# Quartered products: seven products of sums of quarters for eight, weight sums by adding DMAs, and a token-major residual, in a two-layer decoder trunk in float32

## The chip, the cores and the metric

The kernel runs on one core of a Trainium2 chip. TensorE (PE in the rows; its weight loads are PEld) multiplies, VectorE (DVE), ScalarE (ACT) and GpSimd (POOL) work element by element, and SyncE (SP) issues most transfers, which 16 DMA engines carry. The metric is the device time of one execution in microseconds (us), the median of several runs.

## The reference, cut to what matters

There are 512 tokens of width 1024 and two layers. One layer is:

```python
h = rms_norm(x, norm_mix_g[l])
proj = h @ w_in[l]                      # 1024 x 7168: pool 512, q 512, k 512, v 1024, gate 1024, xq 512, 3 branch gates of 1024
y_ret = retention(rq, rk, rv, rg, positions, ret_norm_g[l])       # 4 heads, decaying causal scores, rotary q and k
y_mem = memory_attention(xq, rms_norm(mem, mem_norm_g[l]), w_mem_kv[l])   # 4 heads over 256 memory tokens
y_pool = pool_mixer(pool_u, pool_w[l], pool_scale[l])             # trailing means over 2, 4, 8, 16 tokens
merged = sum over b of sigmoid(gate_b) * (y_b @ w_up_b[l])        # w_up_ret 1024 x 1024, the other two 512 x 1024
x = x + merged @ w_out[l]                                         # 1024 x 1024
h2 = rms_norm(x, norm_mlp_g[l])
x = x + square(relu(h2 @ w_mlp1[l])) @ w_mlp2[l]                  # 1024 x 4096 and 4096 x 1024
```

After the second layer comes a last RMS norm. All data are float32.

## The kernel before

**Exact products in three passes.** Each float32 operand is split into a high part, rounded to the type fp32r that TensorE takes in one pass, and the rest. `split_w` does it for weights: ACT writes `wh` (L120) and DVE `wl = raw - wh` (L121), for 1024 columns at a time. `split` (L99, L100; with a scale L102, L103) does it for activations. `mm` then issues three matmuls for each pair of tiles:

```python
(sh, sl), (mh, ml) = stat, mov
nc.tensor.matmul(ps, sh, mh, start=start, stop=False)     # L127
nc.tensor.matmul(ps, sh, ml, start=False, stop=False)     # L128
nc.tensor.matmul(ps, sl, mh, start=False, stop=stop)      # L129
```

The stationary tile is 128x128; the moving tile has up to 512 columns, and the result goes to one of 8 PSUM banks of 128x512.

**Feature-major products.** The activations lie as 8 tiles `hh`, `hl` of 128 features by 512 tokens. `proj_fm` takes the columns of a weight in groups of 128: per group one bank and, for a depth of 1024, 8 x 3 matmuls with the weights stationary and 512 tokens moving. A product of the whole 1024 x 1024 takes 8 x 8 x 3 = 192 of them:

```python
for j in range(step // P):
    ps = bank()
    for r, raw in enumerate(raws):
        wp = split_w(raw[:, :, j * P:(j + 1) * P])
        for k in range(raw.shape[1]):
            kk = r * 8 + k
            mm(ps[:, :n], tuple(p[:, k, :] for p in wp), xs[kk], kk == 0, kk == kt - 1)
    late.append((c // P + j, ps))
    yield
    if len(late) > lag:
        done(*late.pop(0))
```

`proj_tm` gives token-major results (values, memory values, and the last product), with 128 tokens stationary and 512 weight columns moving. `done` is what follows a bank: the row factor of the norm, the gate, the relu and square (L716, L717, and the split with POOL at L100), or the addition to the residual `xT` (L703), which stays in SBUF feature-major. `Norm` needs its row sums from TensorE (L252) and spreads them over the partitions by two matmuls with diagonal matrices (L275, L276).

**Order.** Weights come by SP's queue in buffers of the pool `wraw` (3 of 1 MB), their parts in `whl` (3). Beside the products run generators in a list `sides` (retention, attention, pooling windows, norms); `run` takes a step of each after every group. A scheduler then sets each engine's order of instructions; every engine works its own in that order and waits by semaphores.

## Time and profile before

| | |
|---|---|
| time, median of 3 runs (lowest, highest) | 1743.9 us (1743.77, 1744.13) |
| span of the profiled execution, first to last instruction | 1741.8 us |
| busy: TensorE / VectorE / ScalarE / GpSimd | 1727.1 / 857.7 / 581.6 / 285.7 us |
| read from HBM / written | 165.88 / 2.10 MB |
| mean granted clock of TensorE | 0.999 of full speed |

The span is what the rows account for. The times agree within 0.4 us, so a change of 0.2% (3.5 us) can be told from none. A matmul's duration in the rows holds its way through the array and overlaps the next one's: the pace is read from start to start.

### The profile page before, as it was taken

What the parts mean: (1) busy time and instruction counts of PE and PEld (TensorE: products, weight loads), DVE (VectorE), ACT (ScalarE), POOL (GpSimd) and SP (SyncE); (2) the same over time, 40 slices, a digit from 0 to 9 for tenths busy, and PEclk for the clock granted to TensorE, in tenths of its full rate; (3) what the DMA queues carried; (4) which work ended last, traced back from release to release, by engine and by line L of the source; (5) the groups of instructions that cost most, each with busy time, mean ns of one, the idle gap of its engine ahead of it and who ended that gap; (6) DMA issues with size and microseconds to landing.
All of it is one profiled execution on the core that took longest, in us unless ns stands there. A gap on an engine that the chain in (4) does not pass through costs nothing.

```text
span 1741.8 us, 19325 instructions
## 1 busy us (share of the span) xinstructions
PE 1727.1 (99%) x7938; PEld 1440.0 (83%) x7938; DVE 857.7 (49%) x1191; ACT 581.6 (33%) x817; POOL 285.7 (16%) x222
## 2 busy tenths in 40 slices
PE   8999999999999999999999999999999999999998
PEld 7788888888888888888888888888888888888886
DVE  6776644644555432443336664456446454235433
ACT  5343334433343321232233333344234332122322
POOL 2312000122022200221122120003110332002210
PEclk9999999999999999999999999999999999999999
DMA  5323224113333223332222232241233332232321
GB/s 198 108 62 97 97 97 145 61 61 122 102 100 94 97 97 97 97 97 97 97 73 85 85 121 86 95 133 61 67 109 115 94 104 100 95 93 91 109 97 49
DMA packets 166184, 169.22 MB, mean 97 GB/s; under 512 B 3208, under 2 KB 153936, under 8 KB 165968
## 3 DMA queue, kind: packets, MB, share of 16 engines
q1 hardware_dynamic: 165504, 167.29, 29.8%
q8 instruction: 62, 1.02, 0.2%
q10 hardware_dynamic: 592, 0.69, 0.1%
q14 instruction: 26, 0.21, 0.0%
HBM read 165.88 MB, written 2.10 MB: 96 GB/s over the span
## 4 chain that ended last, share of the span: by engine, by line
PE 96%; DVE 2%; POOL 1%; DMA 1%; issue 0%; ACT 0%; SPq 0%; POOLq 0%; ACTq 0%; DVEq 0%
PE ps L127 30%; PE ps L128 30%; PE ps L129 30%; PE y L128 1%; PE y L129 1%; PE st L252 1%; PE y L127 1%; PE pt L635 0%; POOL t L445 0%; DMA xin<-in_x 0%; DVE wl L121 0%; PE sc L129 0%; PE sc L128 0%; PE sc L127 0%; PE xs L128 0%
## 5 line engine op out<-in xcount | busy, mean ns | idle before, releaser
L120 ACT CAST wh<-raw 128x1024 fp32r<-128x1024 f32 (+1 forms) x320 | 322.9, 1009 | 860.2 <-PE ps L128 675.4
L121 DVE TENSOR_TENSOR wl<-raw,wh 128x1024 fp32r<-128x1024 f32 (+1 forms) x320 | 382.7, 1196 | 280.9 <-ACT wh L120 279.4
L127 PE MATMUL ps<-hh,wh 128*128 128x512 f32 x1280 | 500.2, 391 | 0.0
L129 PE MATMUL ps<-hh,wl 128*128 128x512 f32 x1280 | 498.4, 389 | 0.0
L128 PE MATMUL ps<-hl,wh 128*128 128x512 f32 x1280 | 498.3, 389 | 0.0
L129 PEld LDWEIGHTS ps<-hh,wl 128*128 128x128 f32 x1280 | 240.3, 188 | 50.3
L127 PEld LDWEIGHTS ps<-hh,wh 128*128 128x128 f32 x1280 | 240.4, 188 | 49.2
L128 PEld LDWEIGHTS ps<-hl,wh 128*128 128x128 f32 x1280 | 240.4, 188 | 48.8
L100 POOL TENSOR_TENSOR actl<-mt,acth 128x512 fp32r<-128x512 f32 x64 | 96.6, 1511 | 424.7 <-ACT acth L99 424.7
L127 PE MATMUL ps<-acth,wh 128*128 128x512 f32 x384 | 149.4, 389 | 0.0
L128 PE MATMUL ps<-actl,wh 128*128 128x512 f32 x384 | 149.4, 389 | 0.0
L129 PE MATMUL ps<-acth,wl 128*128 128x512 f32 x384 | 149.4, 389 | 0.0
L716 DVE TENSOR_TENSOR mt<-ps,rB 128x512 f32<-128x512 f32 x64 | 44.2, 691 | 169.6 <-PE ps L129 169.6
L296 POOL TENSOR_TENSOR sq<-sq 128x512 f32<-128x512 f32 x28 | 47.4, 1694 | 294.3 <-ACT sq L292 294.1
L129 PEld LDWEIGHTS ps<-acth,wl 128*128 128x128 f32 x384 | 72.1, 188 | 15.1
L127 PEld LDWEIGHTS ps<-acth,wh 128*128 128x128 f32 x384 | 72.1, 188 | 14.9
L128 PEld LDWEIGHTS ps<-actl,wh 128*128 128x128 f32 x384 | 72.1, 188 | 14.9
L703 DVE TENSOR_TENSOR xT<-xT,ps 128x512 f32<-128x512 f32 x40 | 27.5, 687 | 114.8 <-PE ps L129 114.8
L515 DVE TENSOR_TENSOR gz<-ps,rB 128x512 f32<-128x512 f32 x48 | 33.0, 688 | 91.8 <-PE ps L129 91.8
L525 DVE TENSOR_TENSOR mt<-ps,gz 128x512 f32<-128x512 f32 x48 | 33.0, 687 | 50.7 <-PE ps L129 50.7
L99 ACT CAST acth<-mt 128x512 fp32r<-128x512 f32 x64 | 39.9, 623 | 47.2 <-DVE mt L717 47.2
L127 PE MATMUL ps<-wh,hh 128*128 128x512 f32 x128 | 51.2, 404 | 0.6 <-DVE sf L479 0.6
(226 smaller groups left out, 2281.9 us busy)
## 6 DMA issues: line engine op xcount, KB each, us to landing
raw<-in_w_mlp SPq DMA_DIRECT2D x64, 1024.0 KB, 5.3
raw<-in_w_in SPq DMA_DIRECT2D x43, 1024.0 KB, 4.9
raw<-in_w_in SPq DMA_DIRECT2D x26, 512.0 KB, 3.7
raw<-in_w_up_ret SPq DMA_DIRECT2D x8, 1024.0 KB, 5.0
raw<-in_w_mem_kv SPq DMA_DIRECT2D x8, 1024.0 KB, 4.8
raw<-in_w_out SPq DMA_DIRECT2D x8, 1024.0 KB, 5.0
raw<-in_w_up_mem SPq DMA_DIRECT2D x8, 512.0 KB, 3.5
raw<-in_w_up_pool SPq DMA_DIRECT2D x8, 512.0 KB, 3.4
```

Source lines behind the costliest of these rows:

```text
L99: nc.scalar.copy(hi, src)
L100: (lo or nc.vector).tensor_tensor(lw, src, hi.bitcast(F32), ALU.subtract)
L120: nc.scalar.copy(hi, view)
L121: nc.vector.tensor_tensor(lw, view, hi.bitcast(F32), ALU.subtract)
L127: nc.tensor.matmul(ps, sh, mh, start=start, stop=False)
L128: nc.tensor.matmul(ps, sh, ml, start=False, stop=False)
L129: nc.tensor.matmul(ps, sl, mh, start=False, stop=stop)
L296: nc.gpsimd.tensor_tensor(self.S, self.S, sq, ALU.add)
L515: nc.vector.tensor_tensor(z, ps, mix.rB, ALU.mult)
L525: nc.vector.tensor_tensor(t, ps, sg.pop(d), ALU.mult)
L703: nc.vector.tensor_tensor(xT[i], xT[i], ps, ALU.add)
L716: nc.vector.tensor_tensor(t, ps, norm2.rB, ALU.mult)
```

## The change

**Products.** A product X W with X in quarters of 256 tokens by half the depth and W in quarters of half the depth by 512 columns is made from seven products of quarters or of sums and differences of quarters (Winograd's form). For X these are, by the numbers in the code: 1: X00, 2: X01, 5: X10 - X11, 6: (5) - X00, 3: X01 + (6), 7: X00 - X10, 4: X11. For W: 1: W00, 2: W10, 5: W00 + W01, 6: (5) + W11, 3: W11, 7: W01 + W11, 4: (6) + W10. Products 1 and 2 share two banks, and 7 and 4 two; `after` recombines the four quarters of the result with one ScalarE copy and five DVE additions for each 128x512. `products` applies it to every large product: per layer seven of `w_in` (the columns of q with k and of xq with pool taken together), `w_up_ret`, `w_out`, four of `w_mlp1` and four of `w_mlp2` at depth 1024, and `w_up_mem` and `w_up_pool` at depth 512. Only the memory's keys and values stay products of the usual kind (`Plain`).

**Passes.** A step is a quarter of W's rows (256 x 512, a buffer of 512 KB) in all its uses. Token-major (`fm=False`) a step is 12 matmuls with 128 tokens stationary and 512 weight columns moving. Feature-major (`fm=True`: q with k, xq with pool, `w_mlp1`) it is 24 with the weights stationary and 256 tokens moving. A product of depth 1024 has 14 steps, one of depth 512 has 7. `push` runs the splits of a step ahead of its matmuls by `LOOK = 2` steps. Product 4 is put off behind product 1 of the next weight, unless `last=True`.

**Weight sums.** At depth 1024 `take` splits a buffer and then has GpSimd issue a DMA that adds the next quarter from HBM to it; there are four such additions in a product, of two buffers each, and three plain quarter loads. At depth 512 GpSimd adds in SBUF (`sums`).

**Activations.** The residual is token-major: `normed` takes the row sums by ACT's accumulator, scales the tokens, and turns them by 32 TensorE transposes of 128x128 (`transposed`) for each norm; the retention's output and the merged branches are turned so too. Branch gates are stored to HBM after their sigmoid and loaded back (`sig`); the residual of the first layer's end likewise (`xsave`).

```diff
-    wraw = ctx.enter_context(tc.tile_pool(name="wraw", bufs=3))
+    wraw = ctx.enter_context(tc.tile_pool(name="wraw", bufs=8))
...
+        def take(self, p, kp):
+            q = self.q
+            if self.n == 2:
+                part, then = {1: ("A", q(0, 1)), 5: ("A", q(1, 1)), 6: ("A", q(1, 0)), 4: ("A", None),
+                              3: ("B", q(0, 1)), 7: ("B", None), 2: ("C", None)}[p]
+                raw = self.buf[part][kp]
+                wp = split_w(raw)
+                if then is not None:
+                    nc.gpsimd.dma_start(raw, rows2(then, kp), accum_op=ALU.add)
+                return wp
...
+            if (p, kp) not in self.sums:
+                eng, x, y, op = {5: lambda: (nc.vector, q[1, 0], q[1, 1], ALU.subtract),
+                                 6: lambda: (nc.vector, self.value(5, kp), q[0, 0], ALU.subtract),
+                                 7: lambda: (nc.gpsimd, q[0, 0], q[1, 0], ALU.subtract),
+                                 3: lambda: (nc.gpsimd, q[0, 1], self.value(6, kp), ALU.add)}[p]()
...
+                if fm:
+                    for c in range(4):
+                        o = bs[c // 2][:, (c % 2) * H:(c % 2 + 1) * H]
+                        for k in range(2):
+                            mm(o, tuple(v[:, k, c * P:(c + 1) * P] for v in wp), tuple(v[:, k, :] for v in xp),
+                               new and kp == 0 and k == 0 and c % 2 == 0, kp == n - 1 and k == 1 and c % 2 == 1)
+                else:
+                    for b in range(2):
+                        for k in range(2):
+                            mm(bs[b], tuple(v[:, k, b * P:(b + 1) * P] for v in xp), tuple(v[:, k, :] for v in wp),
+                               new and kp == 0 and k == 0, kp == n - 1 and k == 1)
...
+                if p == 1:
+                    sb["u", b] = slot(name="u2")
+                    nc.scalar.copy(sb["u", b], ps[1][b])
+                elif p == 2:
+                    done(0, 0, b, ps[1][b], True)
+                elif p == 6:
+                    u = sb["u", b]
+                    v(u, u, ps[6][b], ALU.add)
+                    vv = sb["v", b] = slot(name="vv")
+                    v(vv, ps[5][b], u, ALU.subtract)
+                    c = slot(name="c12")
+                    v(c, vv, ps[3][b], ALU.add)
+                    done(0, 1, b, c, False)
+                elif p == 7:
+                    c = sb["v", b]
+                    v(c, c, ps[7][b], ALU.subtract)
+                    done(1, 1, b, c, False)
+                elif p == 4:
+                    c = sb["u", b]
+                    v(c, c, ps[7][b], ALU.add)
+                    done(1, 0, b, c, False)
...
+        product(1)
+        while late:
+            late.pop(0)()
+        if nxt:
+            nxt.load("A")
+        product(2, 1)
+        if nxt:
+            nxt.load("C")
+        product(5)
+        product(3)
+        product(6)
+        product(7)
+        if nxt:
+            nxt.load("B")
+        if last:
+            product(4, 7)
+        else:
+            late.append(lambda: product(4, 7))
...
+            def done(i, j, b, val, in_psum):
+                x = xt[2 * i + b][j]
+                (nc.vector if in_psum or urgent else nc.gpsimd).tensor_tensor(x, x, val, ALU.add)
```

In an instruction's row here the operands stand as out<-moving,stationary on TensorE and out<-in elsewhere; numbers are buffers. On TensorE the first product of `w_mlp1` begins so before, eight pairs of tiles into one bank:

```order
L127 MATMUL ps_4186<-hh_3913,wh_4187 128x512
L128 MATMUL ps_4186<-hl_3914,wh_4187 128x512
L129 MATMUL ps_4186<-hh_3913,wl_4188 128x512
L127 MATMUL ps_4186<-hh_3949,wh_4187 128x512
L128 MATMUL ps_4186<-hl_3950,wh_4187 128x512
L129 MATMUL ps_4186<-hh_3949,wl_4188 128x512
```

and so now (`x1h`, `x1l` are the parts of X00, `P1` the bank of product 1):

```order
L115 MATMUL P1_6122<-x1h_5187,wh_6074 128x256
L116 MATMUL P1_6122<-x1l_5188,wh_6074 128x256
L117 MATMUL P1_6122<-x1h_5187,wl_6075 128x256
L115 MATMUL P1_6122<-x1h_5187,wh_6074 128x256
L116 MATMUL P1_6122<-x1l_5188,wh_6074 128x256
L117 MATMUL P1_6122<-x1h_5187,wl_6075 128x256
```

Each weight load now serves half as many moving columns. On VectorE the same stretch of `w_mlp2` was weight splits with one addition to the residual after every two:

```order
L121 TENSOR_TENSOR wl_4981<-raw_4917,wh_4980 128x1024
L121 TENSOR_TENSOR wl_5009<-raw_4919,wh_5008 128x1024
L703 TENSOR_TENSOR xT2_92<-xT2_92,ps_4921 128x512
L121 TENSOR_TENSOR wl_5043<-raw_5037,wh_5042 128x1024
L121 TENSOR_TENSOR wl_5071<-raw_5039,wh_5070 128x1024
L703 TENSOR_TENSOR xT3_93<-xT3_93,ps_4979 128x512
```

and is now, between the first step of product 5 and the second of product 3 (`xs5`, `xs6`, `xs3` are the sums of activation quarters, `x5l` and `x3l` low parts, `x` the residual):

```order
L109 TENSOR_TENSOR wl_5875<-raw_5286,wh_5874 128x1024 [waits DMASW0_49,Activation_49]
L102 TENSOR_TENSOR x5l_5871<-xs5_5868,x5h_5870 128x512 [waits Activation_49]
L234 TENSOR_TENSOR xs5_5891<-u2_5358,vv_5663 128x512 [waits DVE_49]
L109 TENSOR_TENSOR wl_5898<-raw_5288,wh_5897 128x1024 [waits DMASW1_49,Activation_49]
L102 TENSOR_TENSOR x5l_5894<-xs5_5891,x5h_5893 128x512 [waits Activation_49]
L895 TENSOR_TENSOR x_4728<-x_4728,P1_5754 128x512 [waits PE_49]
L895 TENSOR_TENSOR x_4732<-x_4732,P1_5755 128x512 [waits PE_49]
L234 TENSOR_TENSOR xs6_5916<-xs5_5868,act_5434 128x512
L109 TENSOR_TENSOR wl_5925<-raw_5670,wh_5924 128x1024 [waits DMAHW1_49,Activation_49]
L109 TENSOR_TENSOR wl_5952<-raw_5672,wh_5951 128x1024 [waits DMAHW2_49,Activation_49]
L102 TENSOR_TENSOR x3l_5921<-xs3_5918,x3h_5920 128x512 [waits Activation_49]
L234 TENSOR_TENSOR xs6_5943<-xs5_5891,act_5437 128x512
```

VectorE makes the sums and splits of the activations in between, and waits there for an adding DMA (DMASW). On GpSimd, which before had one low part after another there (`actl<-mt,acth`, L100), the queue in the same stretch is:

```order
L194 DMA raw_5286<-in_w_mlp2 128x2x512 [waits DMASW0_49,DVE_49]
L194 DMA raw_5288<-in_w_mlp2 128x2x512 [waits DMASW1_49,DVE_49]
L234 TENSOR_TENSOR xs3_5918<-act_5659,xs6_5916 128x512 [waits DVE_49,Pool_49]
L194 DMA raw_5670<-in_w_mlp2 128x2x512 [waits DMAHW1_49,DMASW4_49,DVE_49]
L194 DMA raw_5672<-in_w_mlp2 128x2x512 [waits DMAHW2_49,DMASW5_49,DVE_49]
L234 TENSOR_TENSOR xs3_5945<-act_5667,xs6_5943 128x512 [waits DVE_49,Pool_49]
L194 DMA raw_5286<-in_w_mlp2 128x2x512 [waits DMASW6_49,DMASW2_49,DVE_49]
L194 DMA raw_5288<-in_w_mlp2 128x2x512 [waits DMASW7_49,DMASW3_49,DVE_49]
```

An addition waits for the landing of the one before it in that buffer and for VectorE's split of it, and what stands behind it in GpSimd's order waits too.

## Rows read from the trace of the kernel before

**Rows 1.** The page: busy time, share of the span and instructions of each engine.

```profile
PE 1727.1 (99%) x7938; PEld 1440.0 (83%) x7938; DVE 857.7 (49%) x1191; ACT 581.6 (33%) x817; POOL 285.7 (16%) x222
```

**Rows 2.** The page: the span in 40 slices, busy tenths and granted clock.

```profile
PE   8999999999999999999999999999999999999998
...
PEclk9999999999999999999999999999999999999999
```

**Rows 3.** The page: the chain that ended last, shares by engine.

```profile
PE 96%; DVE 2%; POOL 1%; DMA 1%; issue 0%; ACT 0%; SPq 0%; POOLq 0%; ACTq 0%; DVEq 0%
```

**Rows 4.** Waits, longest in total first: us in total, times, longest.

```profile
ACT wh L120 <- PE ps L128: 679.6, 226, 5.3
```

**Rows 5.** Groups by form, TensorE and ScalarE: busy us, mean ns, idle before.

```profile
L127 PE MATMUL ps<-hh,wh 128*128 128x512 f32 x1280 | 500.2, 391 | 0.0
...
L120 ACT CAST wh<-raw 128x1024 fp32r<-128x1024 f32 x288 | 302.9, 1052 | 787.6 <-PE ps L128 610.5 <-PE ps L129 101.4 <-issue 69.2
```

**Rows 6.** Timeline of TensorE: start us, us, then the instruction; 128x512, then 128x256.

```profile
75.38 0.39 PE L127 MATMUL ps<-hh,wh 128*128 128x512 f32 x1
...
76.06 0.39 PE L127 MATMUL ps<-hh,wh 128*128 128x512 f32 x1
...
266.09 0.28 PE L127 MATMUL ps<-mn,wh 128*128 128x256 f32 x1
...
266.45 0.28 PE L127 MATMUL ps<-mn,wh 128*128 128x256 f32 x1
```

**Rows 7.** The chain that ended last, in order of time: start us, us.

```profile
117.40 0.79 PE st L252 x8
...
320.70 0.87 PE pt L635 x8
```

**Rows 8.** Timeline of VectorE, neighbours without idle time: start us, us.

```profile
42.49 1.23 DVE L121 TENSOR_TENSOR wl<-raw,wh 128x1024 fp32r<-128x1024 f32 x1 [0.22 <-ACT wh L120]
43.63 0.28 DVE L352 CAST ang<-posi 128x256 f32<-128x256 int32 x1
...
602.12 0.69 DVE L717 SCALAR_TENSOR_TENSOR mt<-mt 128x512 f32<-128x512 f32 x1
602.74 1.22 DVE L121 TENSOR_TENSOR wl<-raw,wh 128x1024 fp32r<-128x1024 f32 x1
```

**Rows 9.** Timeline of GpSimd and VectorE, two places where they meet.

```profile
72.48 2.33 POOL L445 TENSOR_TENSOR t<-t,t 128x512 f32<-128x512 f32 x1 [1.50 <-DVE t L444]
...
382.84 1.29 POOL L529 TENSOR_TENSOR mt<-mt 128x512 f32<-128x512 f32 x1 [26.07 <-DVE mt L525]
...
382.98 2.23 DVE L121 TENSOR_TENSOR wl<-raw,wh 128x1024 fp32r<-128x1024 f32 x1 [0.23 <-ACT wh L120]
```

**Rows 10.** DMA: queue's packets, MB, share; issues by line, KB, median us to landing.

```profile
q1 hardware_dynamic: 165504, 167.29, 29.8%
...
raw<-in_w_in SPq DMA_DIRECT2D x43, 1024.0 KB, 4.9
raw<-in_w_in SPq DMA_DIRECT2D x26, 512.0 KB, 3.7
```

**Rows 11.** Timeline of the start: start us, us.

```profile
4.66 1.97 PE L313 MATMUL xtr<-ident,xin 128*128 128x128 f32 x8 [0.68 <-DMA xin<-in_x]
...
8.97 1.63 PE L127 MATMUL ps<-wh,hh 128*128 128x512 f32 x3
```

**Rows 12.** Timeline of the end, and a line of the DMA issues.

```profile
1734.05 0.39 PE L129 MATMUL ps<-wh,actl 128*128 128x512 f32 x1
...
1738.44 0.38 SPq L775 DMA_DIRECT2D out<-xtok  x1
...
out<-fy SPq DMA_DIRECT2D x4, 256.0 KB, 2.0
```

**Rows 13.** Groups by form on VectorE and ScalarE in the softmax.

```profile
L620 DVE TENSOR_REDUCE mx<-xs 128x2 f32<-128x512 f32 x16 | 10.6, 684 | 7.9 <-PE xs L129 7.9
...
L624 ACT ACTIVATE pr<-xs,mx,rsc 128x256 f32<-128x256 f32 x32 | 17.7, 560 | 10.3 <-DVE mx L621 10.3
```

More of the change, by code (lines that the diff above doesn't have):

```diff
@@ L22 @@
 T = 512
+H = 256
 M = 256
@@ new lines, in transposed @@
+    def transposed(x, i, j, kp, src, gain=None):
+        ps = bank("tr")
+        for k in range(2):
+            for b in range(2):
+                nc.tensor.transpose(ps[:, k * H + b * P:k * H + (b + 1) * P],
+                                    src(2 * i + b, j)[:, (2 * kp + k) * P:(2 * kp + k + 1) * P], ident)
+        q = slot(name="q")
+        if gain is None:
+            nc.scalar.copy(q, ps)
+        else:
+            for k in range(2):
+                nc.scalar.mul(q[:, k * H:(k + 1) * H], ps[:, k * H:(k + 1) * H], gain(4 * j + 2 * kp + k))
+        x.q[i, j][kp] = q
@@ new lines, in tile_trunk, with win, full @@
+    for l in range(DEPTH):
+        def win(l, o0, o1):
+            return Weight(lambda i, j: a["w_in"][l][i * T:(i + 1) * T, (o0, o1)[j]:(o0, o1)[j] + T], D)
+        def full(w):
+            K = w.shape[0]
+            return Weight(lambda i, j: w[i * K // 2:(i + 1) * K // 2, j * T:(j + 1) * T], K)
+        plan += [win(l, o, o + T) for o in (OFF_RV, OFF_RQ, OFF_GATE + D, OFF_GATE + 2 * D, OFF_RG, OFF_GATE)]
+        plan.append(win(l, OFF_XQ, OFF_POOL))
+        plan.append(Plain(a["w_mem_kv"][l]))
+        plan += [full(a[n][l]) for n in ("w_up_ret", "w_up_mem", "w_up_pool", "w_out")]
+        for c in range(4):
+            plan.append(full(a["w_mlp1"][l][:, c * D:(c + 1) * D]))
+            plan.append(full(a["w_mlp2"][l][c * D:(c + 1) * D, :]))
@@ new lines, in tile_trunk, with ret_operand, xq_pool @@
+        rop = Operand(2)
+        def ret_operand():
+            for i in range(2):
+                for j in range(2):
+                    while yg[2 * i][j] is None or yg[2 * i + 1][j] is None:
+                        yield
+                    for kp in range(2):
+                        transposed(rop, i, j, kp, lambda t, c: yg[t][c], gain("ret_norm_g", l))
+                    yield
+        xq = {}
+        u = {}
+        mn, km, vm = [], [], []
+        def xq_pool(i, j, b, val, in_psum):
+            if j == 0:
+                xq[i, b] = tuple(two(x) for x in split(val, name="xq"))
+            else:
+                u[i, b] = val
@@ L668, in pool_maps @@
[L668 to L678 removed]
+                mm(ps, tuple(x[:, h * P:(h + 1) * P] for x in vm[m]), pt[m], m == 0, m == NM - 1)
@@ L679, in tile_trunk @@
+        if l == 0:
+            products(hop, v_done)
+            drain()
+        else:
+            products(hop, v_done)
+        products(hop, rotated, fm=True)
+        for hp in range(2):
+            sides.append(retention(hp))
+        products(hop, gate_done(1))
+        products(hop, gate_done(2))
+        while sides:
+            step() if queue else advance()
+        products(hop, swish)
+        sides.append(ret_operand())
+        products(hop, gate_done(0))
         sides.append(memory())
-        run(br)
+        sides.append(pool_weights())
@@ new lines, in tile_trunk @@
+        while late:
+            late.pop(0)()
+        for b in range(2):
+            sides.append(pooling(b))
+        memory_kv()
+        for h in range(HEADS):
+            sides.append(attend(h))
+        products(rop, up_done(1, first=True))
+        flush()
+        drain()
+        products(mop, up_done(2))
+        products(pop, up_done(0, final=True), last=True)
+        if l:
+            xt = x_load(xsave)
+        else:
+            xt = x_load(a["x"][0])
+        count = [0, 0]
@@ L782, in _constants @@
+        for c in range(4):
+            act = Operand(2)
+            products(h2, relu2(act), fm=True)
+            fin = c == 3
+            products(act, add_to_x(end if fin else None, fin), last=fin)
+        flush()
+        drain()
 def _constants():
```

881 lines of the change are left out of this document (436 added, 445 removed).

## The prediction, made before the changed kernel was run

> **What bounds the kernel now.** I read the page's busy line first: TensorE is busy for 99% of the span, VectorE for 49%, ScalarE for 33%, GpSimd for 16% [rows 1]. Busy time of pipelined matmuls proves little, so three more views. The slices show TensorE at nine tenths or more in all but the first and last, at full granted clock, the upper of its two levels, 2.4 GHz [rows 2]. The chain that ended last runs over TensorE for 96% [rows 3], and its commonest group had no idle time before it [rows 5]. The weights' high parts on ScalarE wait for TensorE, 680 us in total: the splits are ahead of the matmuls and held up by buffers that these still read [rows 4]. So a matmul saved is time saved, until something else is late.
>
> The price of a matmul is its pace, not its duration of 0.39 us: three start-to-start steps at 512 columns take 76.06 - 75.38 = 0.68 us, or 0.2266 us each; three at 256 columns take 0.36 us, 0.120 each [rows 6]. A 128x128 transpose costs 0.87 / 8 = 0.109 us, a matmul for the row sums 0.79 / 8 = 0.099 [rows 7].
>
> **The change part by part: TensorE.** A product at depth 1024 was 192 matmuls, 43.5 us.
> - Token-major it is 14 steps of 12, 168 x 0.2266 = 38.1 us: 5.4 less. There are 22 (in a layer `w_up_ret`, `w_out`, four `w_mlp2`, and five of `w_in`): -119.7.
> - Feature-major it is 14 steps of 24 at 256 columns, 336 x 0.120 = 40.3 us: only 3.2 less, since each of twice as many matmuls pays some 13 ns beyond its columns. There are 12: -38.3.
> - At depth 512: 84 x 0.2266 = 19.0 for 21.8. There are 4: -10.9.
> - The old norm's 24 spreading matmuls (5.4) and 96 row sums (9.5) go: -14.9.
> - 192 transposes come (four norms, and per layer retention's output and merged branches, at 32 each, less 64 for input and output before): +20.9.
> - Retention and pooling maps go into 120 more, shorter matmuls at 13 ns: +1.6.
>
> Sum: -161.3. The span of 1741.8 would become 1580.5 if TensorE were fed as well as now.
>
> **VectorE** is what may not feed it. Back to back a weight split takes 43.63 - 42.49 = 1.14 us, a 512-column operation 602.74 - 602.12 = 0.62 [rows 8]. In a product of `w_mlp2` it has now 14 splits (16.0) and 32 wide operations (14 low parts, 4 differences, 10 recombinations, 2 additions to x, 2 relu-squares; 19.8): 35.8 us, beside 38.4 us of TensorE (product 4 of `w_mlp1` falls into it and that of `w_mlp2` out). The mean fits; the order does not quite. When the second activation half of product 5 is split, VectorE has two additions, `xs6`, two weight splits and `x3l` ahead of product 3: 4 x 0.62 + 2 x 1.14 = 4.8 us. TensorE still has the rest of product 5, some 3.0 us. So 1.8 us are lost there. `w_up_ret` and `w_out` carry 36 wide operations, 38.3 us against 38.1: rather 4. I take 3 us for each of the 12 products with a new activation: +36 (bounds 0 and 72).
>
> At depth 512 there are half the splits (8.0), but 27 wide operations for `w_up_mem` (16.7) and 35 for `w_up_pool` (21.7): 24.7 and 29.7 us against 19.0 of matmuls, an excess of 5.7 and 10.7, 33 in two layers. Two steps of lead hide some: +26 (0 to 33).
>
> **Side work.** All four heads of the attention now take each stage in the same step: 8 maxima at 0.62 on VectorE in a row, and 16 exponentials of 0.56 on ScalarE, some 9 us [rows 13], beside two steps of lead (5.4 us) and 5.8 us of score matmuls. I take 6 us a layer: +12 (0 to 30). `flush` empties the lead twice in a layer, a weight split of 1.05 + 1.23 us on two engines each time [rows 5, 8]; and at the two norms the scaled and transposed second half must be ready in products 1 and 2. Together +16 (5 to 30).
>
> **Start and end.** Now the first product starts at 8.97 us, after x by columns [rows 11]. A norm ahead of it needs a million bytes of x, squares, root, scaling, transposes: about 4 later. At the end 4.4 us lie between the last matmul's start and the last store [rows 12]; four squares and a root after the last addition make some 3 more. +7.
>
> **DMA.** The 272 additions (34 products x 8, 512 KB) have no row. As plain transfers they would cost 29.8% of the 16 engines' span for 167.29 MB, 3.1 us a MB: 12.4 us for the 4 MB of a product, beside 9.3 for its 3 MB of plain loads, of about 39 us: hidden. Landing takes at least 3.7 us, as a 512 KB load, and nearer 4.9 with double the bytes moved, as a 1 MB load [rows 10]. The buffer is wanted again four steps on (10.9 us), less a split of 2.3: 8.6 us of room when the splits are just in time. I take these as hidden. Issue on GpSimd is bounded by nothing and by 1.3 us, as a wide operation there [rows 9]; at 1.3 it is 354 us, hidden on an engine busy for 16%.
>
> The Trainium skill (Collectives: The Full Stack, "The bandwidth ceiling: the fold count and why AG ≠ RS ≠ AR") says that an adding DMA reads two sources and so runs at half the rate of a copy. By that the additions of a product would take 24.8 us and all its transfers 34.1 of 39; an estimate, still hidden, but with little left. No run here shows it.
>
> Sum: 1580.5 + 36 + 26 + 12 + 16 + 7 = 1677.5. The runs' median lies 2 above the span: about **1679 us**.
>
> **The rivals.**
> 1. *The products are fed throughout.* The lead of two steps covers VectorE, whose total (520 splits at 1.14, some 1020 wide operations at 0.62, 50 for small ones) is 1275 us, 76% of 1679. For it: TensorE now loses hardly anything where VectorE is two thirds busy. Against it: `w_up_pool` exceeds by its own sum. 1580 + 7 + 5 to 30 for the rest + 2: 1595 to 1630, say 1620.
> 2. *VectorE is the bound of more stages.* It and GpSimd hinder each other: a wide GpSimd operation takes 1.29 or 2.33 us, and a weight split that met one took 2.23 instead of 1.23 [rows 9]. Ten such splits of 320 were long. If each of some 200 wide GpSimd operations costs VectorE 1 us, two thirds of them stand in stages where VectorE is full, and half of that reaches TensorE, this is 200 x 2/3 x 1/2 = 67 more: 1746. The order speaks against it: GpSimd's operations mostly follow one of VectorE's, so VectorE has the next in hand. The Trainium skill (SBUF — State Buffer, "Who interferes with whom") has a VectorE operation with two SBUF inputs and a GpSimd one that reads SBUF shut each other out for the whole operation; the two lengths in the rows agree.
> 3. *Slower: adding DMAs come late.* If an addition takes longer than its 8.6 us of room, each of a product's three uses of a summed quarter of A and one of B waits, and behind the waiting weight split stand the activation splits on ScalarE and VectorE, and so TensorE. Four waits of d us in 34 products cost 136 d: from d = 0.5 the gain of 65 is gone, and 1 us late gives 1815. If additions were 2.6 times as dear as plain bytes, 9.3 + 32 = 41 us a product would fill all DMA engines: the same point as a rate. For it: an unknown price, issued in turn behind GpSimd's other work. Against it: DMA now stands at 30%, and landings at 3.7 and 4.9 us.
>
> **How the numbers follow.** Main case (1635 to 1715) 0.45; rival 1 0.17; rival 2 0.17, in its middle at no change, so two thirds of it faster; rival 3 0.19, nearly all slower; that the form gives no saving at all (the paces do not hold) 0.02. Faster by over 0.2% (about what a measurement here can tell from none): 0.45 + 0.17 + 0.11 + 0.01 = 0.74; within it 0.04; slower 0.22. The range leaves out the best of rival 1 and two thirds of rival 3: 1605 to 1765.
>
> **What would show it.** Right: paces of 0.227 and 0.120; short TensorE gaps ahead of product 3 in `w_mlp2` and in `w_up_mem` and `w_up_pool`, with VectorE's low parts as their releaser; adding DMAs that land in under 8 us. Wrong: weight splits on ScalarE released by DMA (rival 3); many weight splits on VectorE over 2 us (rival 2); TensorE idle for less than 50 us (rival 1); a granted clock that falls in the gaps, which no row here prices.

## The result, and the profile after

The changed kernel takes 2049.9 us (median of four runs, 2047.4 to 2058.8), the kernel before 1743.8 beside it: a ratio of 1.176, with a 95% interval of 1.174 to 1.179. It is slower by 306 us, 371 us over the forecast and outside its range. The profiled execution spans 2048.0 us.

The page of the changed kernel, the parts that answer to [rows 1, 2, 5 and 10]:

```profile
PE 1715.4 (84%) x9282; PEld 1468.3 (72%) x9282; DVE 1480.8 (72%) x1785; ACT 980.0 (48%) x1503; POOL 722.6 (35%) x572
...
PE   5888998997676889999779789889966678999896
...
PEclk9888999998787999999889889999987889999998
...
q0 software_dynamic: 73984, 142.62, 42.4%
q1 hardware_dynamic: 79072, 149.44, 22.3%
...
L109 DVE TENSOR_TENSOR wl<-raw,wh 128x1024 fp32r<-128x1024 f32 x520 | 693.5, 1339 | 327.3 <-ACT wh L108 319.7
...
L194 POOL DMA_DIRECT2D raw<-in_w_in x112 | 135.5, 1212 | 404.4 <-DVE wl L109 342.4
...
raw<-in_w_mlp POOLq DMA_DIRECT2D x128, 512.0 KB, 6.5
raw<-in_w_in POOLq DMA_DIRECT2D x112, 512.0 KB, 6.9
raw<-in_w_mlp SPq DMA_DIRECT2D x96, 512.0 KB, 4.2
```

TensorE has its smaller amount of work, but is no longer fed: 84% busy, and in whole slices six or seven tenths. At the prediction's paces the trace's 4176 matmuls of 512 columns, 4704 of 256 and 400 transposes and small ones come to 946 + 564 + 44 = 1554 us. The same sum for the kernel before is 1713 (7176 of 512 columns, 360 of 256, some 44 us of the rest). So 159 us of matmuls did go, and the time beyond them, the *excess* below, rose from 29 to 494 us. By the page TensorE is idle for 2048.0 - 1715.4 = 333 us of it (before: 15); the other 161 pass with TensorE busy below these paces. Where the busy slices fall, the granted clock falls too: its mean of 0.923 over two levels, 1 and 0.5, is 15% of the span, 315 us, at 1.2 GHz; so the lower clock can directly account for no more than those 161 us.

Six stretches of the changed kernel in the view by windows (us, then busy time and instructions of each engine, granted clock, DMA share): the first gate's product with the retention, the second gate's, the two products of depth 512, `w_out`, the second `w_mlp1` with its `w_mlp2`, and the layer's last `w_mlp2` with the next norm.

```profile
122.70:213.60 90.90, 72.71 (x386) 63.14 (x385) 65.62 (x99) 45.61 (x99) 26.44 (x23) 0.85 0.53 114
213.60:251.70 38.10, 38.10 (x169) 31.55 (x169) 21.05 (x23) 20.23 (x25) 8.60 (x8) 1.00 0.89 211
488.60:587.40 98.80, 64.06 (x225) 47.33 (x225) 82.59 (x95) 31.28 (x44) 33.66 (x19) 0.80 0.40 117
587.40:658.20 70.80, 50.14 (x203) 39.65 (x201) 45.25 (x58) 37.47 (x66) 17.92 (x14) 0.81 0.53 112
746.00:836.50 90.50, 82.30 (x506) 72.68 (x505) 70.94 (x74) 41.50 (x51) 40.07 (x32) 0.98 0.78 163
972.80:1054.10 81.30, 56.04 (x245) 44.81 (x245) 51.80 (x67) 39.74 (x69) 18.70 (x15) 0.83 0.61 146
```

The second row is the form as it was meant: 168 matmuls in 38.1 us, full clock, VectorE half busy, and the DMA engines at 0.89, their highest of the six. In the fifth, the forecast's steady state, the pair takes 90.5 us for 78.4 of matmuls (87.0 before). The rest of the loss lies in stretches where DMA is at its lowest.

What TensorE waits for in `w_out`: the timeline of the changed kernel (start, us, instruction, idle time before it), ScalarE, VectorE and GpSimd, then TensorE.

```profile
617.05 0.62 ACT L101 CAST x7h<-xs 128x512 fp32r<-128x512 f32 x1 [0.50 <-POOL xs L234]
618.22 1.04 ACT L108 CAST wh<-raw 128x1024 fp32r<-128x1024 f32 x1 [0.54 <-PE P L117]
...
618.63 0.68 DVE L102 TENSOR_TENSOR x7l<-xs,x7h 128x512 fp32r<-128x512 f32 x1
...
624.67 0.69 DVE L895 TENSOR_TENSOR x<-x,c 128x512 f32<-128x512 f32 x1
626.15 0.16 DVE L412 TENSOR_TENSOR r<-ss 128x2 f32<-128x2 f32 x1 [0.79 <-ACT sq L410]
...
626.59 0.73 POOL L402 TENSOR_TENSOR r<-r,nhalf 128x2 f32<-128x2 f32 x1 [9.57 <-DVE r L401]
...
617.79 0.39 PE L117 MATMUL P<-wh,x6l 128*128 128x512 f32 x1
628.12 1.97 PE L345 MATMUL tr<-ident,xn 128*128 128x128 f32 x8 [9.95 <-ACT xn L424]
...
633.25 0.78 PE L115 MATMUL P<-wh,x7h 128*128 128x512 f32 x1
633.83 0.63 PE L116 MATMUL P<-wl,x7h 128*128 128x512 f32 x1
```

The last matmul of product 6 starts at 617.8, and the activations of product 7 are split by 619.3. But `normed` writes its transposes into the program at the moment product 6 is recombined, ahead of product 7, and TensorE stands still for 9.95 us until recombination, squares, root and scaling are through. Then product 7 begins at the lower clock (a matmul lasts 0.63 us, where it lasts 0.39 at the upper).

And a place in the steady pair, where `w_mlp2`'s late product 4 meets additions to the residual on GpSimd (same view; GpSimd, VectorE, TensorE):

```profile
839.61 1.75 POOL L895 TENSOR_TENSOR x<-x,c 128x512 f32<-128x512 f32 x1
840.87 2.96 POOL L895 TENSOR_TENSOR x<-x,vv 128x512 f32<-128x512 f32 x2
...
840.18 4.20 DVE L102 TENSOR_TENSOR x4l<-vv,x4h 128x512 fp32r<-128x512 f32 x1
844.31 1.21 DVE L109 TENSOR_TENSOR wl<-raw,wh 128x1024 fp32r<-128x1024 f32 x1
845.44 0.68 DVE L102 TENSOR_TENSOR x4l<-vv,x4h 128x512 fp32r<-128x512 f32 x1
...
842.21 0.39 PE L115 MATMUL P<-wh,x4h 128*128 128x512 f32 x1
845.57 0.67 PE L116 MATMUL P<-wl,x4h 128*128 128x512 f32 x1 [2.97 <-DVE wl L109]
846.04 0.63 PE L117 MATMUL P<-wh,x4l 128*128 128x512 f32 x1
...
849.03 0.45 PE L115 MATMUL P<-wh,x4h 128*128 128x512 f32 x1
849.32 0.39 PE L116 MATMUL P<-wl,x4h 128*128 128x512 f32 x1
```

The same low part takes 4.20 us across three GpSimd additions, ending 0.55 us after the third, and 0.68 without one. The weight split behind it comes late, TensorE idles 2.97 us, and the matmuls behind the wait step by (849.03 - 846.04) / 7 = 0.427 us, for 0.227.

Waits of the changed kernel (us in total, times, longest):

```profile
POOL raw L194 <- DVE wl L109: 817.9, 170, 20.4
...
PE tr L345 <- ACT xn L424: 68.1, 16, 9.9
...
ACT wh L108 <- DMA raw<-in_w_in: 39.2, 19, 2.9
PE P L115 <- ACT x3h L101: 37.4, 28, 6.8
...
PE P L116 <- DVE wl L109: 30.8, 15, 3.9
```

GpSimd's DMA issues wait for VectorE's splits; the splits on ScalarE hardly wait for DMA. TensorE waits for transposes (`tr`), for the high part of product 3's activations (`x3h`) and, in product 4 above all, for low parts of weights (`wl`).

### The profile page after: what moved, and what is told of

Same layout as the page of the kernel before. It is cut to its first block, busy times and chain, and to the rows that moved or that the text cites. A ratio compares the mean times of both kernels' runs of the same rounds, so it can differ in the third digit from the quotient of the medians.

```text
span 2048.0 us, 24869 instructions
## 1 busy us (share of the span) xinstructions
PE 1715.4 (84%) x9282; PEld 1468.3 (72%) x9282; DVE 1480.8 (72%) x1785; ACT 980.0 (48%) x1503; POOL 722.6 (35%) x572
## 3 DMA queue, kind: packets, MB, share of 16 engines
q0 software_dynamic: 73984, 142.62, 42.4%
q1 hardware_dynamic: 79072, 149.44, 22.3%
## 5 line engine op out<-in xcount | busy, mean ns | idle before, releaser
L109 DVE TENSOR_TENSOR wl<-raw,wh 128x1024 fp32r<-128x1024 f32 x520 | 693.5, 1339 | 327.3 <-ACT wh L108 319.7
L108 ACT CAST wh<-raw 128x1024 fp32r<-128x1024 f32 x520 | 545.6, 1050 | 678.9 <-PE P L117 345.7
L194 POOL DMA_DIRECT2D raw<-in_w_in x112 | 135.5, 1212 | 404.4 <-DVE wl L109 342.4
L194 POOL DMA_DIRECT2D raw<-in_w_mlp x128 | 154.1, 1213 | 304.9 <-DVE wl L109 304.3
L115 PE MATMUL P<-wh,x3h 128*128 128x512 f32 x192 | 83.5, 435 | 36.3 <-ACT x3h L101 34.5
L116 PE MATMUL P<-wl,x4h 128*128 128x512 f32 x192 | 83.8, 436 | 20.8 <-DVE wl L109 20.8
L115 PE MATMUL P<-wh,x1h 128*128 128x512 f32 x192 | 81.1, 422 | 14.1 <-ACT x1h L101 14.1
L115 PE MATMUL P<-wh,x4h 128*128 128x512 f32 x192 | 82.8, 432 | 11.1 <-ACT x4h L101 3.4
L117 PE MATMUL P<-wh,x4l 128*128 128x512 f32 x192 | 82.7, 432 | 1.0 <-DVE x4l L102 1.0
L115 PE MATMUL P<-wh,x7h 128*128 128x512 f32 x192 | 80.9, 421 | 2.5 <-ACT x7h L101 2.5
```

The lines of the kernel that those rows point to most:

```text
L108: nc.scalar.copy(hi, raw)
L109: nc.vector.tensor_tensor(lw, raw, hi.bitcast(F32), ALU.subtract)
L115: nc.tensor.matmul(ps, sh, mh, start=start, stop=False, skip_group_check=True)
L116: nc.tensor.matmul(ps, sh, ml, start=False, stop=False, skip_group_check=True)
L117: nc.tensor.matmul(ps, sl, mh, start=False, stop=stop, skip_group_check=True)
L194: nc.gpsimd.dma_start(raw, rows2(then, kp), accum_op=ALU.add)
```

## The experiments

The letters name theories, whose prices stand in each expectation. Theory A, formed on this profile: four things add up: operations that stand too early in an in-order queue, wide GpSimd operations that shut out VectorE, sums at depth 512, and the clock that falls in each gap. Its rivals are the prediction's third, adding DMAs, and VectorE's plain total. Lengths of some stages (us, from first matmul to first matmul; "branches" are the three `w_up` products, "pair" the second `w_mlp1` and `w_mlp2`, "layer end" the last `w_mlp2` and the norm behind it, all of the first layer):

| stage | changed | e2 | e3 | e4 | e8 | e12 | e17 |
|---|---|---|---|---|---|---|---|
| two gates, retention | 129.0 | 128.9 | 129.3 | 129.3 | 127.8 | 121.0 | 115.7 |
| branches | 150.4 | 143.2 | 132.3 | 108.7 | 105.0 | 108.1 | 100.0 |
| `w_out`, first `w_mlp1` | 115.7 | 106.1 | 112.5 | 116.7 | 96.4 | 87.7 | 91.1 |
| pair | 90.5 | 81.4 | 90.5 | 91.6 | 81.4 | 79.0 | 79.0 |
| layer end | 81.3 | 78.8 | 59.6 | 81.0 | 59.0 | 55.0 | 52.2 |

**e1: no additions of weights.**

```diff
-                if then is not None:
+                if then is not None and False:
```

> The 272 adding DMAs are left out, so five of the seven weight quarters of a depth-1024 product are used unsummed; everything else stays. Theory A (TensorE waits in its own order for norms and transposes, VectorE and GpSimd shut each other out, and the clock falls in the gaps; the additions are off the path): GpSimd loses 272 x 1.2 us of issues that nothing waits for, and ScalarE's weight splits wait for DMA for 39 us in all: 1990 to 2050 us. Theory B (rival 3 of the prediction: the additions come late or fill the DMA engines): the whole loss goes, 1650 to 1750 us.

Measured: 1988.8 us (ratio 1.140, 1.138 to 1.142), 61 less. Theory B falls: with no addition at all the kernel is still 14% slower than before. Theory A's interval is missed by 1 us.

**e2: wide sums off GpSimd** (two of the places in the diff; e7 is this kernel once more: 1949.1 us).

```diff
-                             7: lambda: (nc.gpsimd, q[0, 0], q[1, 0], ALU.subtract),
-                             3: lambda: (nc.gpsimd, q[0, 1], self.value(6, kp), ALU.add)}[p]()
+                             7: lambda: (nc.vector, q[0, 0], q[1, 0], ALU.subtract),
+                             3: lambda: (nc.vector, q[0, 1], self.value(6, kp), ALU.add)}[p]()
```

> The same arithmetic, with GpSimd's wide additions moved: the activation sums xs3 and xs7, the additions to the residual, the rotary sum, the swish product and the merged branches to VectorE, the squares after relu to ScalarE. GpSimd keeps the DMA issues, the pooling windows and the depth-512 weight sums. Theory A (a wide GpSimd operation and a VectorE one shut each other out: 168 us of VectorE's time beyond the shortest tenth of each form, all of it where a GpSimd operation overlaps): VectorE gets some 150 operations of 0.68 us, 100 us, and loses most of the 168; the waits behind GpSimd (ScalarE's x3h and x7h, 130 us) go too: 1900 to 1980 us. Theory C (VectorE's total is what TensorE waits for): VectorE's work grows by 100 us and the time stays or rises, 2040 to 2120 us.

Measured: 1948.1 us (1.116, 1.114 to 1.119), 102 less. VectorE now has 152 more instructions and is busy for 42 us less than the 1480.8 of the changed kernel. The page and groups of e2 and then, below, groups of the changed kernel (busy, mean ns):

```profile
PE 1676.0 (86%) x9282; PEld 1448.2 (75%) x9282; DVE 1439.1 (74%) x1937; ACT 1002.8 (52%) x1535; POOL 442.1 (23%) x388
...
L109 DVE TENSOR_TENSOR wl<-raw,wh 128x1024 fp32r<-128x1024 f32 x520 | 648.6, 1250 | 301.3 <-ACT wh L108 285.8 <-DMA pw<-in_pool_w 11.9 <-issue 1.9
...
L102 DVE TENSOR_TENSOR x4l<-vv,x4h 128x512 fp32r<-128x512 f32 x16 | 10.9, 689 | 6.8 <-ACT x4h L101 6.8
```

```profile
L102 DVE TENSOR_TENSOR x6l<-xs,x6h 128x512 fp32r<-128x512 f32 x36 | 54.0, 1527 | 3.3 <-ACT x6h L101 3.3
...
L102 DVE TENSOR_TENSOR x4l<-vv,x4h 128x512 fp32r<-128x512 f32 x16 | 31.8, 1996 | 6.8 <-ACT x4h L101 6.8
```

The mean `x4l` falls from 1996 to 689 ns and the weight split from 1339 to 1250, 45 us over 520 of them. VectorE's total (theory C) is not the bound. How the 102 us divide between VectorE's longer operations, GpSimd's slower sums and their lateness in its queue was not tried apart.

**e9: e2 without the additions** (the edit of e1 on e2).

> The kernel of e2 (sums off GpSimd, 1948 us) without the adding DMAs; as in e1, five of seven weight quarters stay unsummed. In e1 leaving them out gave 61 us. Theory A (there it was GpSimd's queue: xs3, xs7 and the additions to the residual stood behind DMA issues that wait for VectorE's split; with these sums on VectorE nothing stands behind them): 1935 to 1950 us. Theory B (it is the transfers themselves: landing and load of the DMA engines): 1880 to 1900 us, the same 61 less.

Measured: 1930.8 us (1.107, 1.105 to 1.109), 17 less than e2 and 4 past theory A's end. So 17 of e1's 61 us at most are the transfers; the other 44 go only while GpSimd also has the wide sums, which stand behind issues of 1.21 us that wait for VectorE. That its queue is the cause is argued from this difference and from rows of e1:

```profile
PE P L116 <- DVE wl L109: 4.1, 4, 2.2
...
L102 DVE TENSOR_TENSOR x4l<-vv,x4h 128x512 fp32r<-128x512 f32 x16 | 18.2, 1144 | 6.8 <-ACT x4h L101 6.8
```

Without the issues ahead of them the sums meet VectorE's low parts of product 4 less (a mean of 1144 ns for 1996), and TensorE's waits for weight splits fall from 30.8 to 4.1 us. The issues by themselves do not lengthen VectorE's work: its weight split has a mean of 1252 ns in e9 without them and of 1250 in e2 with them. Together the two edits save 119 us, not 61 + 102, so the 44 us stand in e2's 102 too.

**e3: transposes later.** `normed` and the branches hand their transposes to `defer`, which runs them a set number of steps on:

```diff
+    def defer(n, f):
+        deferred.append([n, f])
...
-            for kp in range(2):
-                transposed(x, i, c, kp, lambda t, c: xn[t % 2, c], g)
+        defer(3, turn)
```

> Only TensorE's order changes: the transposes of a norm's token half (and of the merged branches) stand some steps later, behind products that do not need them (the first half's behind products 7 and 4, the second half's behind products 1 and 2 of the next weight), and the lead is not emptied between the layers. Theory A (these transposes stand ahead of ready matmuls; gaps of 38 us a layer ahead of them in w_out and w_up_pool and 20 at the first layer's end, 97 in all, and 37 us of matmuls at the lower clock there): 1910 to 1965 us. Theory C (the norm's work on VectorE and ScalarE is the bound, wherever the transposes stand): the gaps move to the next weight splits, 2020 to 2050 us.

(Here the second token half of the second layer's first norm took the gain of another norm.) Measured: 1994.3 us (1.144, 1.142 to 1.146), 56 less: direction and places as theory A had them (layer end 81.3 to 59.6, branches 150.4 to 132.3), size short by 29 to 84 us. A part of it came back at once: the first `w_mlp1` takes 51.9 us for 44.9, since it now waits for what the norm makes.

**e4: depth 512 by eight products.**

```diff
+        if n == 1:
+            return usual(x, done, w, nxt)
```

> w_up_mem and w_up_pool alone go back to eight products of quarters: four weight splits a product, 96 matmuls of 512 columns for 84, no weight sums on GpSimd, no recombination. Their two stages take 42 and 56 us for 22 and 25 us of matmuls, 98.8 in the first layer. Theory A (VectorE's and GpSimd's work on sums is the bound of these two): matmuls grow by 11 us in all four, the excess falls by 50 to 70: 1980 to 2010 us. Theory D (the loss there is the waiting for gates loaded back and for transposes): 2040 to 2065 us.

Measured: 1971.0 us (1.130, 1.128 to 1.132), 79 less, more than either theory had, though matmuls grow by 11.

**e5: sides in turn.**

```diff
-        for hp in range(2):
-            sides.append(retention(hp))
+        sides.append(heads(retention, 0, 1))
...
-        for h in range(HEADS):
-            sides.append(attend(h))
+        sides.append(heads(attend, 0, 2))
+        sides.append(heads(attend, 1, 3))
```

> As the changed kernel, but the two retention generators run one after the other, not in the same steps, and the four attention heads in two pairs of chains. The stage of the second gate has 14 steps without any lost time (38.1 us for 38.0 of matmuls), that of the first, where both retentions start, loses 31 and 33 us. Theory A (side work comes in bursts of 13 us of VectorE in two steps, while neighbouring products have room): 1985 to 2025 us. Theory C (VectorE's total is the bound): within 5 us of 2050.

Measured: 2051.3 us (1.175, 1.174 to 1.177): no change, as theory C has it. The first gate's stage falls from 90.9 to 71.7 us, the second's grows from 38.1 to 57.3, and `w_up_ret` with the attention from 51.6 to 55.1. Theory A falls for the retention: spreading its bursts only moved the loss.

**e6: the clock held up.**

```diff
+            if at and c == 0:
+                fill(FILLN[i])
             for kp in range(2):
                 transposed(x, i, c, kp, lambda t, c: xn[t % 2, c], g)
```

> As the changed kernel, with matmuls of zeros (256 columns, into a bank that nobody reads) put ahead of the transposes of norms and of the merged branches, where TensorE waits: 68 and 40 for a norm's halves, 52, 36, 1 and 20 for the merged branches. No wait is taken away; TensorE only has something to do in it. Theory A (part of the loss is the fall of the granted clock to 1.2 GHz in gaps: 46 us of matmuls' own pace stand at the lower clock in w_up_pool, w_out, the first stage of w_mlp1 and the last of w_mlp2): 2005 to 2030 us. Theory E (the clock costs nothing beyond the gaps themselves): 2050 to 2065 us, the fillers being in the way where they last longer than the wait.

Measured: 2038.1 us (1.168, 1.167 to 1.170), 12 less, between the two theories. Windows of e6, to lay beside the changed kernel, whose clock is 0.78 in the same 62 us and 0.81 in the 60 before:

```profile
540.00:600.00 60.00, 49.34 (x263) 42.13 (x262) 48.77 (x63) 23.80 (x34) 16.31 (x11) 0.94 0.51 130
600.00:662.00 62.00, 53.67 (x322) 47.16 (x321) 40.50 (x53) 35.13 (x64) 13.65 (x12) 0.94 0.47 104
```

The mean clock rises from 0.923 to 0.940 without one wait taken away: the fall comes with the gaps and has a price of its own. Its whole price this run does not give, since the clock was only partly held and the added matmuls take time too.

**e8: e2 to e5 together.**

> The edits of e2 (sums off GpSimd), e3 (transposes later, here with the right gain for the second layer's first norm), e4 (depth 512 by the usual products) and e5 (sides in turn) together. If their savings add up (102, 56, 79 and, by its expectation, 45): about 1770 us. If TensorE's losses are behind one common bound, VectorE's total, less: 1850 to 1950 us. Below 1744 only if, beyond the sum, the clock stays up where gaps no longer fall together.

Measured: 1822.5 us (1.045, 1.043 to 1.046), between the two expectations. By the measured savings, 102 + 56 + 79 and nothing for e5, 1813 was due: they add up within 10 us, so they are different losses.

**e10: eight products in e8's kernel.** `products` runs the four quarters of the result one after the other, weights come by plain loads, and the norms' transposes stand six steps on, not three:

```diff
+        for i, j in ((0, 0), (0, 1), (1, 1), (1, 0)):
+            for c in range(2):
+                for kp in range(n):
```

> The kernel of e8 (1822.5 us) with eight products of quarters in place of seven in all large products: 16 steps of one quarter of the weight each, loaded by plain DMAs (each quarter twice), no sums of weights or activations, no recombination; the token-major residual, the transposes, the sides and 256-column moving tiles in the feature-major products stay. Matmuls at their pace grow by 22 x 5.4 + 12 x 5.8 = 189 us, from 1561 to 1750. Theory F (what is lost beyond the matmuls' pace, 261 us in e8, belongs to the new stages: start, norms, retention, attention, end; the seven products themselves gain): 1890 to 1970 us. Theory G (it belongs to the seven products' sums and recombination on VectorE): the 261 fall below 80 us and the time stays at 1790 to 1840 us.

Measured: 1854.3 us (1.063, 1.062 to 1.065): under theory F's range and over G's. The pages of e8 and of e10:

```profile
PE 1655.2 (91%) x9330; PEld 1441.2 (79%) x9330; DVE 1358.2 (75%) x1857; ACT 974.3 (53%) x1503; POOL 401.2 (22%) x372
...
PEclk7999999999999999999989899999999999999998
```

```profile
PE 1783.5 (96%) x10434; PEld 1581.1 (85%) x10434; DVE 1132.8 (61%) x1377; ACT 1005.4 (54%) x1475; POOL 59.1 (3%) x100
...
PEclk9999999999999999999999999999999999999999
```

By the same paces e10's 4752 matmuls of 512 columns and 5280 of 256 come to 1754 us, e8's 4224 and 4704 to 1565. With eight products the excess is 1852.0 - 1754 = 98 us, with seven 1821.6 - 1565 = 256. In this structure, then, seven for eight saves 189 us of matmuls and gives back 158 in waits. And the structure itself, eight products in both, costs 110 us against the kernel before: 41 of matmuls (256-column pieces, transposes) and 69 of excess. TensorE's longest waits in e10 stand at the start (some 25 us) and ahead of the pooling's maps and of the retention's products with the values (some 11 each).

**e11 and e12: a lead of three steps** (with the rotary tables in smaller steps and the values split earlier, as the expectation says).

```diff
-LOOK = 2
+LOOK = 3
```

> The kernel of e8 with a lead of three steps for two (a fourth pair of split weight buffers, 72 slots for 76), the rotary tables made three operations a step, and the split of the values ahead of the retention's scores. Theory A (what is left in e8 are short waits of TensorE for work that comes a step late: x3h 23 us, the values' high parts 17 us, and the clock that falls there): 1770 to 1800 us. Theory H (they are waits of whole chains, norm and retention, that a lead of weights does not shorten): 1810 to 1825 us.

Measured: 1840.6 us, 18 worse than e8, outside both theories. The timeline of e11, TensorE in `w_mlp2`:

```profile
621.57 0.39 PE L117 MATMUL P<-wh,x2l 128*128 128x512 f32 x1
629.60 0.79 PE L115 MATMUL P<-wh,x5h 128*128 128x512 f32 x1 [7.64 <-ACT x5h L101]
```

`get` splits an operand when its step is prepared, if it exists by then, and otherwise only when its matmuls are written. Three steps ahead product 5's operand does not yet exist, and its split came with its matmuls.

```diff
+        for cut in list(cuts):
+            if cut[0] <= 0 or cut[1]():
+                cuts.remove(cut)
```

> The kernel of e11 (1840.6 us) with one edit: an activation operand that does not exist yet when its step is prepared is split as soon as a later step has made it, not just ahead of its matmuls. In e11 each w_mlp2 stage has one gap of 7.7 us ahead of product 5, whose operand comes from the late product 4 of w_mlp1, prepared three steps ahead when that is not yet done, and takes 48.7 us for 41.4 in e8. Theory A (that is all that the longer lead made worse): eight stages give 7.3 us each, 1775 to 1790 us. Theory I (the longer lead costs by its 72 slots or its order elsewhere): 1800 to 1840 us.

Measured: 1764.9 us (1.011, 1.010 to 1.013), 76 less than e11 and better than theory A, which had 58 for the gaps of `w_mlp2` alone; the edit splits every late operand early, not only theirs. The pair now takes 79.0 us for 78.4 of matmuls, with VectorE busy for 65.2 of them.

**e13 to e15: places that stand too early.** e13 hands the first norm's second half and the transposes of the other gains to `defer`, and ends only the side work (`while sides: step()`) where `flush()` emptied the lead:

```diff
-        if at == 0:
+        if at == 0 and i == 0:
             turn()
...
-        flush()
-        drain()
+        while sides:
+            step() if queue else advance()
```

> The kernel of e12 (1764.9 us) with two places changed: at the start the transposes of the first norm's second token half stand behind products 1 and 2 (in e12 TensorE waits 9.6 us for them and 5.8 us for the other gains' rows, whose transposes now come seven steps later), and before the attention and before the depth-512 products only the side work is finished, not the lead emptied (gaps of 1.8 and 3.3 us there in each layer). Theory A (each gap is work that stands too early in an in-order queue): 12 to 16 us at the start, 8 to 12 in the two layers: 1735 to 1748 us. Theory H (the chains behind it are the bound): above 1755 us.

> The kernel of e13, and the side work gets steps between what makes an operand and the matmuls that read it: one ahead of the retention's products with the values (a gap of 4.3 us in each layer), the second retention nine steps behind the first, two ahead of the transposes of the memory (5 us), one between the pooling's splits and its matmuls (2.5 and 1.1 us). Theory A: 13 us of gaps a layer and some 4 of matmuls at the lower clock behind them: 25 to 34 us less than e13. Theory H: within 8 us of e13.

> The kernel of e14, with the small operations of a norm's root on GpSimd and its scaling on ScalarE alone, so that VectorE does not stand still for ScalarE's sums of squares while a weight split waits behind (gaps of 2.5 to 4.8 us ahead of product 4 in w_out and in each layer's last w_mlp2). Theory A: 10 to 18 us less than e14. Rival (ScalarE, which then scales four tiles in a row and waits for the root, holds up the weights' high parts instead): no change or up to 10 us more.

Measured: e13 1747.8 us (1.0023, 1.0013 to 1.0033), theory A; e14 1749.3 (1.0027, 1.0017 to 1.0036), theory H: the gaps ahead of the values' products went (9.9 us in the two layers) and others came ahead of product 6 (8.4 us), with VectorE behind; e15 1764.5, 15 worse than e14 and outside both expectations. In e15's trace the issue of an addition stands between the two steps of a root, whose power takes 2.59 us for 0.73 in the changed kernel; whether that is all of the 15 us was not tried.

**e16 and e17: the norms in another place, then the retention later.**

```diff
-        r = row_factors(xt, i)
+        defer(2, scale)
...
             while len(qk) < 8:
                 yield
+            if not hp:
+                yield
+                yield
```

> The kernel of e13 (1747.8 us) with the norms' work in another place: each tile of the residual is squared when it is final, not all four when the last is, and the root and scaling of a token half stand two steps later, behind the recombination of product 7. In e13 VectorE stands still for a norm's sums while product 7's result waits in PSUM behind it, and product 4 waits for that bank (gaps of 4.0 and 4.6 us with the clock falling behind them, six norm halves in three norms). Theory A (VectorE's order): 12 to 22 us less, 1726 to 1736 us. Rival (the norm's chain is the bound and only moves the gap to its transposes): 1743 to 1750 us.

> The kernel of e16, and the retention starts two steps later and has one step more ahead of its products with the values, so that VectorE has finished the rotary products of q and k (22 us) before TensorE asks for scores. In e13 the stage of the first gate loses 21 and 19 us. Theory A: 6 to 12 us less than e16. Theory C (VectorE's total in this stage is the bound, as e5 and e14 suggested): within 4 us of e16.

Measured: e16 1751.1 us (1.0045, 1.0033 to 1.0057), the rival, 1 us past its end: the gap ahead of product 4 in `w_out` falls from 3.8 to 2.3 us, and the one ahead of the second half's transposes grows from 0.9 to 3.6. e17 1740.6 us (0.9979, 0.9971 to 0.9988), 10.5 less than e16, as theory A had it: a part of the retention's loss was its place in the order, not VectorE's total. Which of e17's two steps, the later start or the one ahead of the products with the values, gave it was not tried apart. It is the only version here below the kernel before, by 0.2%. Its page:

```profile
PE 1625.1 (93%) x9330; PEld 1422.7 (82%) x9330; DVE 1355.3 (78%) x1857; ACT 972.8 (56%) x1503; POOL 392.4 (23%) x372
```

Its profiled execution, the slowest of its eleven runs, spans 1744.2 us, 179 over the 1565 of its matmuls, for 29 before: of the 148 us of matmuls that it saves (depth 512 has eight products again) almost all is still given back.

## Why the prediction was wrong, step by step

The sum had 36 + 26 + 12 + 16 + 7 = 97 us of losses against 161 saved; the excess in fact rose by 465.

- **TensorE, -161.** Right: 159 by count and pace, and 0.227 and 0.120 hold where it is fed (168 matmuls in 38.1 us; pair of e12 in 79.0).
- **VectorE in products with a new activation, +36.** Undersized, and only partly in the right place: TensorE waited ahead of product 3, as said (37.4 us for `x3h`), but also in the late product 4, which the sum did not have (30.8 us for weight splits, most of it there). In the pair it is 90.5 - 78.4 = 12.1 us, not 3 a product. The failed step is that the main sum priced VectorE's operations at 0.62 and 1.14 us whatever GpSimd does beside it, and set rival 2 aside with: "The order speaks against it: GpSimd's operations mostly follow one of VectorE's, so VectorE has the next in hand." A next operation in hand is just what meets GpSimd's. Rival 2's sign came: 39 of the 520 weight splits lasted over 2 us (7 of 320 before). e2 puts this at 102 us, GpSimd's own lateness included; rival 2 had 67. The Trainium skill (SBUF — State Buffer, "Who interferes with whom") has the two engines' shared port pair as an exclusive lock; the 4.20 us and their 0.68 in e2 agree.
- **Flush and boundaries, +16.** This step failed most plainly. I priced the norm as work that must be ready in the next product, and did not look where its transposes stand: ahead of product 7, whose operands lie ready. One such place cost 9.95 us of idling and then the clock of product 7's first matmuls. Moving them, and those of the merged branches, gave 56 us (e3), the start and the lead another 17 (e13).
- **Depth 512, +26 (0 to 33).** Undersized: the two products took 98.8 us in the first layer, for some 47 of matmuls (22 and 25 with the late product 4 and the transposes among them), and putting back the usual form gave 79 us in all with 11 us more matmuls. VectorE was busy for 82.6 of them, where I had summed 54, and the lead of two steps that was to hide a part is emptied by `flush` before them and held up by transposes inside them (e3 took 18 us from the branches; e13 took 8 more from the usual form).
- **Attention, +12.** Inside its range: `w_up_ret` with the attention took 51.6 us for some 42 of matmuls. The retention was given nothing for stalls, without a reason, and its stage lost 31 us in a layer (90.9 for some 60 of matmuls); e17's places took back 5 of them, the rest of the reason is not settled.
- **Start and end, +7.** Undersized: the first product starts at 30.2 us, not 13, for two norm halves and a second set of gains stand ahead of it; 11 us lie behind the last matmul's start, not 7. The 4 and 3 us that the term was made of came from no row.
- **Adding DMAs hidden, rival 3.** The transfers: nearly right. They land in 6.5 to 6.9 us, later than the 3.7 to 4.9 taken but under the 8.6 of room and the 8 named, and ScalarE's weight splits waited 42 us for loads in all. The issue: sized right (1.21 us, under the bound of 1.3), but "hidden on an engine busy for 16%" was judged by the busy share and not by the order: an issue waits for VectorE's split (817.9 us in all), and the sums behind it wait too. That is how the 44 of e1's 61 us are read here. By the two queues' rows an added MB takes 42.4 / 142.62 against 22.3 / 149.44, 2.0 times a plain one. The Trainium skill (Collectives: The Full Stack, "The bandwidth ceiling: the fold count and why AG ≠ RS ≠ AR") has a collective's adding step at half the rate of its copying one, because the addition reads two sources; the page speaks of rings of cores, and the 2.0 of these adding loads on one core agrees with its ratio.
- **The clock.** Named as unpriced, which was the gap in the range: 315 us of the span stood at 1.2 GHz. What it cost by itself is settled only in bounds: at most 161 us of the excess are TensorE busy below its pace, and e6 took back 12 us for 0.017 of the mean clock.

The range failed because its cases took each loss alone, on a TensorE that had never waited; they add up (e8), and behind gaps such as the 9.95 and 2.97 us shown above the matmuls start at the lower clock.

Left open: what divides the last 179 us of e17 between the norms' own chains and VectorE's order at the stage borders. e14 and e16 only moved it, e15 added to it.

## What to carry to other kernels

A form that saves matmuls and pays in element-wise work must be judged from the order on each in-order engine, not from sums: write down what stands ahead of the first ready matmul at every stage border. Wide sums given to an idle GpSimd are not free when VectorE is the busy engine beside it; and an operand that is split "ahead" is only ahead if it exists when that step is prepared. Here the best version saves 148 us of matmuls and is 0.2% faster.

## What the runs showed of the hardware

- An adding DMA of 512 KB holds GpSimd for 1.21 us to issue, lands 6.5 to 6.9 us later (a plain load of the same size: 4.2 to 4.7), and costs 2.0 times as much of the DMA engines per MB.
- One VectorE low part of 128x512 lasted 4.20 us across three GpSimd additions, six times its 0.68.
- After an idle time of 2.97 us the matmuls stepped at the lower level of the clock (seven steps of 0.427 us, for 0.227); with matmuls of zeros in the waits the mean granted clock of a 62 us stretch was 0.94, where it had been 0.78.
